# Seven quarter products in place of eight for the gate and up products of two swiglu stages

## The chip, the cores and the metric

The kernel runs on one core of a Trainium2 chip. The core has a matrix engine (TensorE, PE in the profile; its weight loads are listed apart as PEld), a vector engine (VectorE, DVE), a scalar engine (ScalarE, ACT), a general engine (GpSimd, POOL) and a sync engine that issues the weight transfers (SyncE, SP). Each engine works through its own list of instructions in order, and waits at an instruction until the semaphores that it names are set. The metric is device time in microseconds (us) of one execution; shown is the median of three runs.

## The reference

Two transformer blocks on 512 tokens of width 1024, in float32. Block 1 has two kinds of sparse attention and a squared-relu feed-forward; block 2 has a swiglu, a mixing stage (stick-breaking attention and an RWKV-7 recurrence), and a second swiglu. The change touches the two swiglus:

```python
def swiglu(x, w_gate, w_up, w_down):
    return (jax.nn.silu(x @ w_gate) * (x @ w_up)) @ w_down

x = x + FFN_HALF * swiglu(rms_norm_2(x, norm_ffn1[l]), ffn1_gate[l], ffn1_up[l], ffn1_down[l])
...
x = x + FFN_HALF * swiglu(rms_norm_2(x, norm_ffn2[l]), ffn2_gate[l], ffn2_up[l], ffn2_down[l])
```

`w_gate` and `w_up` are 1024 x 2816, `w_down` is 2816 x 1024.

## The kernel before

Activations lie transposed: eight tiles `x[0..7]` of 128 features by 512 tokens. Every float32 operand of a big product is split in two parts, an upper part rounded to the matrix format (ACT copies it: `whi`, `hh`, `vh`) and the rest as a lower part (DVE subtracts: `wlo`, `hl`, `vl`). A product is then three matmuls for each 128 x 128 block of weights: upper by upper, upper by the activations' lower part, lower by upper, in this order (`dense`, lines 352 to 360).

A swiglu stage (`swiglu`, lines 1410 to 1454) has 22 column groups of 128, each with one transfer of 1 MB (a unit): 1024 columns of gate and 1024 of up, 128 for each of the eight feature tiles. They come in three runs of 8, 8 and 6 units (`FFG`). A unit is 2 x 8 x 3 = 48 matmuls of 512 columns. Its two PSUM results are multiplied on DVE with the row scale `rr` (the norm's root, which is ready only some us after the stage begins, so the products run on unscaled activations), go through silu on ACT, are multiplied, and split into `vh` and `vl`. After each run come eight products with `w_down` (8 x 24, 24 or 18 matmuls), added into `x` on DVE.

The weights pass through the class `Stream`: two buffers of 1 MB (`NB = 2`), filled by SP in the order of use. A buffer is free again when the lower part of its last piece is done. `get` hands over one split piece of 1024 columns, and converts at most one further piece ahead (`LA = 1`); the split pieces lie in two buffers each of `whi` and `wlo`. Each engine's order is set by a scheduler ahead of the run, so an engine's list is not the order of the Python lines alone.

GpSimd has no instruction in the swiglu stages.

```python
            for _ in ks:
                if q == 0 and len(u) == 1:
                    for _ in steps:
                        pass
                    pg, pu = nx, self.bank("s")
                    self.dense(pu, ws.get(), h)
                else:
                    pg, pu = self.bank("mm"), self.bank("mm")
```

## Time and profile before

| | |
|---|---|
| median of three runs | 1954.82 us (1954.04 to 1955.6) |
| the profiled execution, its own time | 1951.49 us |
| its span from first to last instruction | 1949.7 us |
| mean granted TensorE clock | 0.979 of full speed |
| busy: PE, PEld | 1864.8 us (96%), 1456.1 us (75%) |
| busy: DVE, ACT, POOL | 1094.1 us (56%), 797.5 us (41%), 149.9 us (8%) |

Busy time is the time in which an engine had at least one instruction running. Matmuls are pipelined: the next starts before the one before has ended, so the time that one costs is the distance between starts, not its own length. The first swiglu lies from about 780 to 1134 us of the span, the second from about 1585 to the end.

### The profile page before, as it was taken

The page shows a single profiled execution, that of the slowest core. Times are in us where ns is not written, and L with a number is a line of the kernel's source. Part 1 is how long each engine was busy: PE and PEld are TensorE (multiplying, and loading weights), DVE is VectorE, ACT ScalarE, POOL GpSimd, SP SyncE. Part 2 cuts the span into 40 slices and gives each one's busy share as a digit, 9 for nine tenths or more (in the row PEclk, how much of TensorE's full clock was granted, in tenths as well). Part 3 has the DMA queues.
Part 4 walks back from the last instruction along what each step waited for, and adds up shares of the span by engine and source line. Part 5 has one row for each costly group of instructions (what it writes and reads, how often), then busy time and mean ns, then how long its engine had stood idle before and what let it go on. Part 6 is the DMA issues. An engine that isn't in the chain of part 4 may idle for free.

```text
span 1949.7 us, 27795 instructions
## 1 busy us (share of the span) xinstructions
PE 1864.8 (96%) x11552; PEld 1456.1 (75%) x11556; DVE 1094.1 (56%) x1843; ACT 797.5 (41%) x1385; POOL 149.9 (8%) x117
## 2 busy tenths in 40 slices
PE   5989999979999998999999999999999999999999
PEld 2766666758888886788888877776766778888887
DVE  7588875583434345543444556676667774444343
ACT  3666767343323233322322354343445753223231
POOL 4341110050000002000000000000001300000000
PEclk8999999889999998999999999999999999999999
DMA  7124214312223221222232231110100022222222
GB/s 300 57 87 140 78 65 152 113 61 92 103 90 105 89 106 65 87 93 101 88 107 87 89 124 55 45 45 24 40 18 33 22 87 96 99 92 103 92 98 92
DMA packets 27486, 171.56 MB, mean 88 GB/s; under 512 B 3168, under 2 KB 3680, under 8 KB 9184
## 3 DMA queue, kind: packets, MB, share of 16 engines
q1 hardware_dynamic: 23472, 163.44, 24.2%
q10 hardware_dynamic: 3888, 6.34, 1.0%
q8 instruction: 91, 1.49, 0.3%
q14 instruction: 35, 0.29, 0.0%
HBM read 167.67 MB, written 2.10 MB: 87 GB/s over the span
## 4 chain that ended last, share of the span: by engine, by line
PE 77%; DVE 3%; ACT 2%; POOL 1%; issue 1%; DMA 1%; ACTq 0%; POOLq 0%
PE ps_mm L339 43%; PE ps_s L339 23%; PE ps_c L339 5%; PE ps_pt L339 4%; PE ps_o L339 1%; ACT whi L243 1%; DVE wlo L249 1%; POOL xr L1332 0%; PE ps_pt L902 0%; POOL x L1381 0%; DMA mask<-in_mask 0%; DMA x<-in_x 0%; PE ps_mm L758 0%; DVE hl L1396 0%; DVE rs_v L510 0%
## 5 line engine op out<-in xcount | busy, mean ns | idle before, releaser
L243 ACT ACTIVATE whi<-w 128x1024 fp32r<-128x1024 f32 (+4 forms) x277 | 274.7, 994 | 740.7 <-PE ps_mm L339 440.8
L339 PE MATMUL ps_mm<-hh,whi 128*128 128x512 f32 x1304 | 519.9, 400 | 20.9 <-ACT whi L243 9.5
L339 PE MATMUL ps_mm<-hh,wlo 128*128 128x512 f32 x1304 | 518.1, 398 | 6.2 <-DVE wlo L249 6.2
L339 PE MATMUL ps_mm<-hl,whi 128*128 128x512 f32 x1304 | 519.2, 398 | 3.4 <-DVE hl L1339 2.0
L249 DVE TENSOR_TENSOR wlo<-w,whi 128x1024 fp32r<-128x1024 f32 (+7 forms) x316 | 322.3, 1025 | 149.3 <-ACT whi L243 148.8
L339 PEld LDWEIGHTS ps_mm<-hh,whi 128*128 128x128 f32 x1304 | 247.6, 190 | 82.3 <-ACT whi L243 12.8
L339 PEld LDWEIGHTS ps_mm<-hh,wlo 128*128 128x128 f32 x1304 | 247.4, 190 | 65.0 <-DVE wlo L249 10.1
L339 PEld LDWEIGHTS ps_mm<-hl,whi 128*128 128x128 f32 x1304 | 247.4, 190 | 60.3 <-DVE hl L1339 3.5
L339 PE MATMUL ps_s<-vl,whi 128*128 128x512 f32 x352 | 137.2, 390 | 0.0
L339 PE MATMUL ps_s<-vh,wlo 128*128 128x512 f32 x352 | 137.0, 389 | 0.0
L339 PE MATMUL ps_s<-vh,whi 128*128 128x512 f32 x352 | 136.6, 389 | 0.0
L1449 DVE SCALAR_TENSOR_TENSOR x<-ps_s,x 128x512 f32<-128x512 f32 x48 | 33.2, 692 | 129.2 <-PE ps_s L339 129.2
L1437 DVE TENSOR_TENSOR su<-ps_mm,rr 128x512 f32<-128x512 f32 x42 | 29.0, 691 | 133.1 <-PE ps_mm L339 133.1
L339 PE MATMUL ps_s<-uh,whi 128*128 128x512 f32 x256 | 99.6, 389 | 0.0
L339 PE MATMUL ps_s<-ul,whi 128*128 128x512 f32 x256 | 99.6, 389 | 0.0
L339 PE MATMUL ps_s<-uh,wlo 128*128 128x512 f32 x256 | 99.6, 389 | 0.0
L1436 DVE TENSOR_TENSOR sg<-ps_mm,rr 128x512 f32<-128x512 f32 x42 | 29.1, 692 | 97.3 <-PE ps_mm L339 93.2
L339 PEld LDWEIGHTS ps_s<-vl,whi 128*128 128x128 f32 x352 | 66.1, 188 | 14.3 <-DVE vl L783 0.7
L339 PEld LDWEIGHTS ps_s<-vh,wlo 128*128 128x128 f32 x352 | 66.1, 188 | 13.7
L339 PEld LDWEIGHTS ps_s<-vh,whi 128*128 128x128 f32 x352 | 66.1, 188 | 13.7
L876 ACT ACTIVATE P<-ps_s,st 128x512 f32<-128x512 f32 (+2 forms) x96 | 50.1, 528 | 15.7 <-DVE st L874 13.8
L1373 DVE TENSOR_TENSOR y<-y,ps_s 128x512 f32<-128x512 f32 x24 | 16.5, 688 | 70.0 <-PE ps_s L339 70.0
(576 smaller groups left out, 2762.5 us busy)
## 6 DMA issues: line engine op xcount, KB each, us to landing
w<-in_gu SPq DMA_DIRECT2D x44, 1024.0 KB, 4.8
w<-in_win SPq DMA_DIRECT2D x17, 1024.0 KB, 4.9
w<-in_wada SPq DMA_DIRECT2D x16, 1024.0 KB, 5.5
w<-in_wup SPq DMA_DIRECT2D x16, 1024.0 KB, 4.8
w<-in_wdn SPq DMA_DIRECT2D x16, 1024.0 KB, 4.8
w<-in_dn SPq DMA_DIRECT2D x16, 1024.0 KB, 4.8
wa<-in_wada SPq DMA_DIRECT2D x8, 1024.0 KB, 13.5
w<-in_dn SPq DMA_DIRECT2D x8, 768.0 KB, 4.2
```

The costliest lines, as they stand in the source:

```text
L243: self.nc.scalar.activation(hi[:, :n], src, AF.Copy)
L249: self.nc.vector.tensor_tensor(lo[:, o:m], src[:, o:m], hi[:, o:m], op=OP.subtract)
L339: self.last_pe = self.nc.tensor.matmul(o, l, r, start=start, stop=stop, skip_group_check=True)
L876: nc.scalar.activation(p[:, po:po + n], b[:, o:o + n], AF.Exp, bias=st[:, i:i + 1], accum_out=st[:, 4 + i:5 + i])
L1373: V.tensor_tensor(y[m], y[m], ps, op=OP.add)
L1436: V.tensor_tensor(g, pg, r, op=OP.mult)
L1437: V.tensor_tensor(v, pu, r, op=OP.mult)
L1449: V.scalar_tensor_tensor(self.x[m], ps, 0.5, self.x[m], op0=OP.mult, op1=OP.add)
```

## The change

The first three units of each swiglu stage stay as they were (`PLAIN = 3`). The other 19 take gate and up as one 2 x 2 block product: the weights of a unit are four quarters of 512 columns, A11 and A12 (gate, first and second four feature tiles), A21 and A22 (up), and the activations are four blocks, first and second four feature tiles by first and second 256 tokens. Seven products of quarter size take the place of eight. Of 48 matmuls of 512 columns come 7 x 4 x 3 = 84 of 256 columns.

The operands of the seven products are sums. Per unit GpSimd forms four weight sums of 512 columns (`combine`: S1, S2, S3, S4), from two SBUF tiles each. Once per stage, in the time of the plain units, `build` makes the activation operands in four steps: two scaled tiles on DVE (`h32`), four sums of 256 columns on GpSimd (`traw`, one buffer), three upper parts on ACT (`b1h`, `b2h`, `bth`) and three lower parts on DVE (`b1l`, `b2l`, `btl`: 256, 512 and 1024 columns). The scale `rr` is in them already, so the PSUM results need no multiplication with it. The results are put together from PSUM with three copies of 256 columns on ACT and three additions of 256 on DVE; the product with silu is two DVE instructions of 256. Weights are split in pieces of 512, seven a unit in place of two of 1024, up to four ahead (`LW = 3`), into the eight `hh`/`hl` tiles that held the activations of the plain units.

```diff
+PLAIN, LW = 3, 3
+            elif chunks == "W":
+                self.items += [(u, w, w == "A22") for w in ("A11", "A12", "S2", "S1", "S3", "S4", "A22")]
...
+    def combine(self, u):
+        if u in self.combos or self.sp is None:
+            return
+        q = lambda n: self.tiles[u][:, 512 * n:512 * n + 512]
+        s = self.combos[u] = {n: self.sp.tile([128, 512], F32, name="sw", tag="sw", bufs=4) for n in ("S1", "S2", "S3", "S4")}
+        for o, a, b, op in (("S1", q(2), q(3), OP.add), ("S2", s["S1"], q(0), OP.subtract), ("S3", q(0), q(2), OP.subtract),
+                            ("S4", q(1), s["S2"], OP.subtract)):
+            self.nc.gpsimd.tensor_tensor(s[o], a, b, op=op)
     def _convert(self):
-        while len(self.ready) <= self.la:
+        while True:
             while self.cp < len(self.items) and self.items[self.cp][1] is None:
                 self.cp += 1
             if self.cp >= len(self.items):
                 return
-            u, (off, n), last = self.items[self.cp]
-            if u >= self.dma_i:
+            u, ch, last = self.items[self.cp]
+            w = isinstance(ch, str)
+            if u >= self.dma_i or len(self.ready) > (LW if w else self.la) or w and self.sp is None:
                 return
-            src = self.tiles[u][:, off:off + n]
-            hi = self.phl.tile([128, 1024], F32R, name="whi")
-            lo = self.phl.tile([128, 1024], F32R, name="wlo")
+            if w:
+                self.combine(u)
+                a = ("A11", "A12", "A21", "A22")
+                src, n = self.tiles[u][:, 512 * a.index(ch):512 * a.index(ch) + 512] if ch in a else self.combos[u][ch], 512
+            else:
+                off, n = ch
+                src = self.tiles[u][:, off:off + n]
+            hi, lo = self.htile() if w else [self.phl.tile([128, 1024], F32R, name=n) for n in ("whi", "wlo")]
...
+            if ch == "S4" and isinstance(self.items[self.cp + 1][1], str) and u + 1 < self.dma_i:
+                self.combine(u + 1)
...
-                e += [(a[f"gu{n}"][u], c2) for u in ks]
+                e += [(a[f"gu{n}"][u], c2 if u < PLAIN else "W") for u in ks]
...
+    def seven_operands(self, pool, name, r):
+        V, S, P = self.nc.vector, self.nc.scalar, self.nc.gpsimd
+        two = lambda nm, *n: [pool.tile([128, 4, *n], F32R, name=nm + x) for x in "hl"]
+        b1, b2, t = two("b1", 256), two("b2", 512), two("bt", 4, 256)
+        def build(k):
+            hs = []
+            for m in (k, k + 4):
+                h = self.tmp("h32")
+                V.scalar_tensor_tensor(h, self.x[m], self.vec(name, m), r, op0=OP.mult, op1=OP.mult)
+                hs.append(h)
+            h1, h2 = hs
+            raw = pool.tile([128, 4, 256], F32, name="traw", tag="traw", bufs=1)
+            lo, hi = slice(0, 256), slice(256, 512)
+            P.tensor_tensor(raw[:, 0], h1[:, hi], h1[:, lo], op=OP.subtract)
+            P.tensor_tensor(raw[:, 1], h2[:, hi], raw[:, 0], op=OP.subtract)
+            P.tensor_tensor(raw[:, 2], h2[:, hi], h1[:, hi], op=OP.subtract)
+            P.tensor_tensor(raw[:, 3], h2[:, lo], raw[:, 1], op=OP.subtract)
+            for (oh, ol), src in ((b1, h1[:, lo]), (b2, h2), (t, raw)):
+                S.activation(oh[:, k], src, AF.Copy)
+                V.tensor_tensor(ol[:, k], src, oh[:, k], op=OP.subtract)
+        pick = lambda p, c: [(p[0][:, k][:, c], p[1][:, k][:, c]) for k in range(4)]
+        comb = lambda i: [(t[0][:, k, i], t[1][:, k, i]) for k in range(4)]
+        lo, hi = slice(0, 256), slice(256, 512)
+        ops = dict(P1=pick(b1, lo), P2=pick(b2, lo), P6=comb(1), P5=comb(0), P7=comb(2), P3=pick(b2, hi), P4=comb(3))
+        return ops, build
+    def seven(self, ops, x, z):
+        V, S, ws = self.nc.vector, self.nc.scalar, self.ws
+        lo, hi = slice(0, 256), slice(256, 512)
+        X, Y, Z = x[:, lo], x[:, hi], z[:, lo]
+        def prod(n, o, start=False):
+            wh, wl = ws.get()
+            for k, (xh, xl) in enumerate(ops[n]):
+                c = slice(128 * k, 128 * k + 128)
+                self.mm(o, wh[:, c], xh, start=start and k == 0)
+                self.mm(o, wh[:, c], xl)
+                self.mm(o, wl[:, c], xh, stop=k == 3)
+        s, s5, a, b = (self.tmp(n) for n in ("s12", "s5", "sg", "su"))
+        prod("P1", X, True)
+        S.activation(s[:, lo], X, AF.Copy)
+        prod("P2", Z, True)
+        V.tensor_tensor(a[:, lo], Z, s[:, lo], op=OP.add)
+        prod("P6", X)
+        S.activation(s[:, hi], X, AF.Copy)
+        prod("P5", Y)
+        S.activation(s5[:, lo], Y, AF.Copy)
+        prod("P7", X)
+        V.tensor_tensor(b[:, hi], X, s5[:, lo], op=OP.add)
+        prod("P3", Y)
+        V.tensor_tensor(a[:, hi], Y, s[:, hi], op=OP.add)
+        prod("P4", X)
+        return a, b, X
     def swiglu(self, h, out=None):
         tc, nc, ws = self.tc, self.nc, self.ws
         V, S = nc.vector, nc.scalar
         es = ExitStack()
         fp = es.enter_context(tc.tile_pool(name="fp2", bufs=1))
-        self.rpool = fp
+        self.rpool = ws.sp = fp
+        ws.htile = self.htile
         r = None
+        name = "norm_ffn1_2" if out is None else "norm_ffn2_2"
+        n = 0
         for q, ks in enumerate(FFG):
             u = []
             for _ in ks:
-                if q == 0 and len(u) == 1:
-                    for _ in steps:
-                        pass
-                    pg, pu = nx, self.bank("s")
-                    self.dense(pu, ws.get(), h)
+                n += 1
+                if n > PLAIN:
+                    g, v, X = self.seven(ops, self.bank("mm"), self.bank("s"))
+                    self.last_silu = S.activation(g, g, AF.Silu)
+                    V.tensor_tensor(v[:, :256], X, g[:, :256], op=OP.mult)
+                    V.tensor_tensor(v[:, 256:], v[:, 256:], g[:, 256:], op=OP.mult)
                 else:
-                    pg, pu = self.bank("mm"), self.bank("mm")
-                    if r is None:
-                        self.dense2(pg, pu, h)
-                        nx = self.bank("s")
-                        steps = self.dense_steps(h, ps=nx)
-                        r = self.gr(steps)
+                    if n == 2:
+                        build(0)
+                        for _ in steps:
+                            pass
+                        pg, pu = nx, self.bank("s")
+                        self.dense(pu, ws.get(), h)
+                        build(1)
                     else:
-                        self.dense(pg, ws.get(), h)
-                        self.dense(pu, ws.get(), h)
-                g, v = self.tmp("sg"), self.tmp("su")
-                V.tensor_tensor(g, pg, r, op=OP.mult)
-                V.tensor_tensor(v, pu, r, op=OP.mult)
-                self.last_silu = S.activation(g, g, AF.Silu)
-                V.tensor_tensor(v, v, g, op=OP.mult)
+                        pg, pu = self.bank("mm"), self.bank("mm")
+                        if r is None:
+                            self.dense2(pg, pu, h)
+                            nx = self.bank("s")
+                            steps = self.dense_steps(h, ps=nx)
+                            r = self.gr(steps)
+                            ops, build = self.seven_operands(fp, name, r)
+                        else:
+                            self.dense(pg, ws.get(), h)
+                            build(2)
+                            self.dense(pu, ws.get(), h)
+                            build(3)
+                    g, v = self.tmp("sg"), self.tmp("su")
+                    V.tensor_tensor(g, pg, r, op=OP.mult)
+                    V.tensor_tensor(v, pu, r, op=OP.mult)
+                    self.last_silu = S.activation(g, g, AF.Silu)
+                    V.tensor_tensor(v, v, g, op=OP.mult)
```

The scheduler gives these lists. First, the vector engine at the start of the first swiglu, from the first instruction that needs `rr_5935`. `w32_5848` is the third unit's weights, `wlo_5966` and `wlo_6006` (before), `wlo_5987` and `wlo_6042` (after) the lower parts of its gate and up halves; `h32`, `b1l`, `b2l`, `btl` belong to `build`. Before, from the second instruction that needs it:

```order
L1437 TENSOR_TENSOR su_5943<-ps_mm_5843,rr_5935 128x512
L1436 TENSOR_TENSOR sg_5993<-ps_s_5898,rr_5935 128x512
L249 TENSOR_TENSOR wlo_5966<-w32_5848,whi_5965 128x1024
L1439 TENSOR_TENSOR su_5943<-su_5943,sg_5942 128x512
L783 TENSOR_TENSOR vl_5949<-su_5943,vh_5948 128x512
L1437 TENSOR_TENSOR su_5994<-ps_s_5964,rr_5935 128x512
L1439 TENSOR_TENSOR su_5994<-su_5994,sg_5993 128x512
L249 TENSOR_TENSOR wlo_6006<-w32_5848,whi_6005 128x1024
```

After, from the first lower part of a build that needs a GpSimd sum:

```order
L1454 TENSOR_TENSOR btl_5947<-traw_5962,bth_5946 128x1024
L805 TENSOR_TENSOR vl_5955<-su_5949,vh_5954 128x512
L1443 SCALAR_TENSOR_TENSOR h32_6014<-x1_2989,vecs_80,rr_5935 128x512
L1443 SCALAR_TENSOR_TENSOR h32_6016<-x5_2993,vecs_80,rr_5935 128x512
L1454 TENSOR_TENSOR b1l_5943<-h32_6014,b1h_5942 128x256
L1534 TENSOR_TENSOR sg_6029<-ps_s_5898,rr_5935 128x512
L1454 TENSOR_TENSOR b2l_5945<-h32_6016,b2h_5944 128x512
L1535 TENSOR_TENSOR su_6030<-ps_s_5985,rr_5935 128x512
L1454 TENSOR_TENSOR btl_5947<-traw_6018,bth_5946 128x1024
L1537 TENSOR_TENSOR su_6030<-su_6030,sg_6029 128x512
L269 TENSOR_TENSOR wlo_6042<-w32_5848,whi_6041 128x1024
```

The lower part of the third unit's up half (`wlo_6006`, now `wlo_6042`) was the ninth instruction from the first that needs `rr`, and is now the nineteenth: it stands behind two builds, and so behind two `btl` that need sums from GpSimd.

Second, GpSimd at the same place. Before, its list goes from the last addition into `x` in block 1 to the attention of block 2, which is after the swiglu:

```order
L1381 TENSOR_TENSOR x4_2992<-x4_2992,y4_3011 128x512
L1381 TENSOR_TENSOR x5_2993<-x5_2993,y5_3012 128x512
L1381 TENSOR_TENSOR x6_2994<-x6_2994,y6_3013 128x512
L1381 TENSOR_TENSOR x7_2995<-x7_2995,y7_3014 128x512
```

After, the weight sums of the fourth unit (`w32_5921`) stand ahead of and between the first build's sums:

```order
L243 TENSOR_TENSOR sw_6047<-w32_5921 128x512
L243 TENSOR_TENSOR sw_6048<-sw_6047,w32_5921 128x512
L1448 TENSOR_TENSOR traw_5962<-h32_5958 128x256
L243 TENSOR_TENSOR sw_6049<-w32_5921 128x512
L1449 TENSOR_TENSOR traw_5962<-h32_5960,traw_5962 128x256
L1450 TENSOR_TENSOR traw_5962<-h32_5960,h32_5958 128x256
L1451 TENSOR_TENSOR traw_5962<-h32_5960,traw_5962 128x256
L243 TENSOR_TENSOR sw_6050<-w32_5921,sw_6048 128x512
L1448 TENSOR_TENSOR traw_6018<-h32_6014 128x256
```

So two sums that need the fourth unit's transfer come ahead of the first build, and the second build's sums wait for DVE to have read the first's from the one `traw` buffer.

Third, the vector engine within a run of seven-product units, about one unit's worth (after; `hl` is a weight's lower part, `sw` a GpSimd sum, the 256-wide rows with `ps_` read PSUM):

```order
L269 TENSOR_TENSOR hl_6556<-sw_6482,hh_6555 128x512
L805 TENSOR_TENSOR vl_6434<-su_6301,vh_6433 128x512
L269 TENSOR_TENSOR hl_6585<-sw_6481,hh_6584 128x512
L269 TENSOR_TENSOR hl_6602<-sw_6483,hh_6601 128x512
L269 TENSOR_TENSOR hl_6619<-sw_6484,hh_6618 128x512
L1487 TENSOR_TENSOR su_6442<-ps_mm_6437,s5_6440 128x256
L269 TENSOR_TENSOR hl_6644<-w32_6365,hh_6643 128x512
L1489 TENSOR_TENSOR sg_6441<-ps_mm_6437,s12_6439 128x256
L269 TENSOR_TENSOR hl_6663<-w32_6506,hh_6662 128x512
L1511 TENSOR_TENSOR su_6442<-su_6442,sg_6441 128x256
L1510 TENSOR_TENSOR su_6442<-ps_mm_6437,sg_6441 128x256
L1481 TENSOR_TENSOR sg_6582<-ps_s_6579,s12_6580 128x256
```

Weights of the next one or two units are converted between the additions that put a unit's result together.

## Rows read from the trace of the kernel before

**Rows 1.** The page: busy time, share of the span and instructions of each engine
```profile
PE 1864.8 (96%) x11552; PEld 1456.1 (75%) x11556; DVE 1094.1 (56%) x1843; ACT 797.5 (41%) x1385; POOL 149.9 (8%) x117
```

**Rows 2.** Chain that ended last, by time: start us, us, what; gate-and-up runs
```profile
796.70 65.28 PE ps_mm L339 x288
...
905.50 87.04 PE ps_mm L339 x384
...
1036.06 65.28 PE ps_mm L339 x288
...
1608.44 65.28 PE ps_mm L339 x288
```

**Rows 3.** One run by engine: PE, PEld, DVE, ACT, POOL, clock, DMA share, GB/s
```profile
905.00:992.00 87.00, 87.00 (x386) 72.03 (x385) 39.11 (x46) 25.57 (x31) 0.00 (x0) 1.00 0.29 97
```

**Rows 4.** Timeline of PE: first and last of thirty 348-column matmuls (start, us)
```profile
63.28 0.32 PE L339 MATMUL ps_s<-whi,hh 128*128 128x348 f32 x1
...
67.85 0.32 PE L339 MATMUL ps_o<-whi,hl 128*128 128x348 f32 x1
```

**Rows 5.** Timeline of PE: first and last of fifteen 32-column matmuls, weights changing
```profile
150.25 0.26 PE L339 MATMUL ps_s<-kcb,qst 128*128 128x32 f32 x1
...
151.82 0.26 PE L339 MATMUL ps_s<-kcb,qst 128*128 128x32 f32 x1
```

**Rows 6.** Timeline of PE: a 256-column matmul and its successor
```profile
1464.58 0.28 PE L339 MATMUL ps_c<-u,negones 128*128 128x256 f32 x1
1464.70 0.22 PE L339 MATMUL ps_c<-tok,negones 128*128 128x128 f32 x1
```

**Rows 7.** First swiglu, by shape: count | busy us, mean ns | idle before, releaser
```profile
L249 DVE TENSOR_TENSOR wlo<-w,whi 128x1024 fp32r<-128x1024 f32 x54 | 66.0, 1223 | 7.1 <-ACT whi L243 7.1
L243 ACT ACTIVATE whi<-w 128x1024 fp32r<-128x1024 f32 x55 | 58.4, 1062 | 204.6 <-PE ps_mm L339 135.3 <-PE ps_s L339 67.4 <-issue 1.9
L782 ACT ACTIVATE vh<-su 128x512 fp32r<-128x512 f32 x20 | 12.7, 634 | 13.6 <-DVE su L1439 13.6
```

**Rows 8.** Timeline of POOL, two successors; then one line's min/median/max ns
```profile
61.27 1.29 POOL L813 TENSOR_TENSOR rp_t<-rp_t,rp_s 128x512 f32<-128x512 f32 x1
62.51 1.30 POOL L812 TENSOR_TENSOR rp_s<-rp_s,sin 128x512 f32<-128x512 f32 x1
...
L1564 POOL TENSOR_TENSOR u<-tmt,u x2: 744/832/919, 1455.5 to 1519.7; 128x256 fp32r<-128x256 f32 x2
```

**Rows 9.** Timeline of POOL, then DVE, where both are busy
```profile
410.00 13.71 POOL L1344 TENSOR_TENSOR x<-x,y 128x512 f32<-128x512 f32 x8
...
412.21 2.54 DVE L1362 TENSOR_TENSOR relu<-relu 128x512 f32<-128x512 f32 x2 [0.86 <-ACT relu L1361]
414.68 2.28 DVE L249 TENSOR_TENSOR wlo<-w,whi 128x1024 fp32r<-128x1024 f32 x1
416.88 3.44 DVE L783 TENSOR_TENSOR ul<-relu,uh 128x512 fp32r<-128x512 f32 x2
420.25 2.32 DVE L249 TENSOR_TENSOR wlo<-w,whi 128x1024 fp32r<-128x1024 f32 x1
```

**Rows 10.** Timelines of ACT and DVE around the scale's arrival, both stages
```profile
790.59 0.60 ACT L1407 ACTIVATE rr<-ps_pt 128x512 f32<-128x512 f32 x1 [1.90 <-PE ps_pt L339]
...
784.90 1.22 DVE L249 TENSOR_TENSOR wlo<-w,whi 128x1024 fp32r<-128x1024 f32 x1
786.04 0.68 DVE L573 TENSOR_TENSOR st<-st,sq 128x512 f32<-128x512 f32 x1
...
791.22 0.69 DVE L1436 TENSOR_TENSOR sg<-ps_mm,rr 128x512 f32<-128x512 f32 x1 [1.94 <-ACT rr L1407]
791.83 0.68 DVE L1437 TENSOR_TENSOR su<-ps_mm,rr 128x512 f32<-128x512 f32 x1
...
798.08 1.22 DVE L249 TENSOR_TENSOR wlo<-w,whi 128x1024 fp32r<-128x1024 f32 x1
...
1600.28 0.60 ACT L1407 ACTIVATE rr<-ps_pt 128x512 f32<-128x512 f32 x1 [2.77 <-PE ps_pt L339]
```

**Rows 11.** The page: DMA issues (count, KB each, us from issue to landing)
```profile
w<-in_gu SPq DMA_DIRECT2D x44, 1024.0 KB, 4.8
```

More of the change, by code (lines that the diff above doesn't have):

```diff
@@ L221, in __init__ @@
         self.pool = 0
+        self.sp, self.combos, self.htile = None, {}, None
     def load(self):
@@ L1453, in swiglu @@
                     nc.scalar.dma_start(out[m], self.x[m])
+        ws.sp = None
         es.close()
```

## The prediction

> **What bounds the kernel now.** I read the busy times first: the matrix engine is at work for 96% of the span, and no other engine comes near [rows 1]. Then the chain of waits, in order of time. The reader is to see that a run of gate and up products stands in it as one unbroken piece of matmuls: 288, 384 and 288 in the first swiglu, and the same three again in the second [rows 2]. 65.28 / 288 and 87.04 / 384 both give 226.7 ns a matmul, or 48 x 0.2267 = 10.88 us a unit. Third, one run by engine: in 87 us TensorE is busy throughout at its full clock (1.00, the 2.4 GHz level), DVE for 39.1, ACT for 25.6, GpSimd not at all [rows 3]. So within a run only matmuls count, and the other engines have room. At the beginning of a stage the margin is smaller, because the row scale arrives late [rows 10].
>
> **The matmuls.** 38 units change (19 in each of two stages). Each gives up 48 matmuls of 512 columns for 84 of 256. No stream of 256-column matmuls is in the trace, so I bound the price. A stream of 348 columns with a weight change at each runs at (67.85 - 63.28) / 29 = 157.6 ns [rows 4]. With 226.7 ns at 512 this is a line of 0.4212 ns a column and a fixed part of 11 ns, which gives 118.8 ns at 256. From below: a fixed part of nothing, half of 226.7 = 113.3. From above: the whole excess of 226.7 over 213.3 (512 columns at 2.4 GHz) as a fixed part, 106.7 + 13.4 = 120. A single one among others takes 0.12 us [rows 6]. Does the weight load set a floor? With 32 columns and a new weight block each time the distance is (151.82 - 150.25) / 14 = 112 ns [rows 5]; that is the load's pace, and lies just under all three. I take 119: 84 x 0.119 = 10.0 us a unit, 0.88 less than now, 33.6 us over 38 units (52 and 30 at the ends).
>
> The Trainium skill (TensorE: Matmul & The Clock Gate, section Back-to-back issue gap) gives a gap of N / 2.4 + 2.5 ns; by it 256 columns would take 109 ns, a unit 9.2, and the whole change 65 us less. It also gives 216 ns for 512, where this trace has 226.7, so its fixed part is too small here and the sum does not use it.
>
> **The other engines within a run.** DVE's instructions follow each other at 0.61 us for 512 columns (791.22 to 791.83) and 1.14 for 1024 (784.90 to 786.04) [rows 10], so about 0.35 for 256. A unit now has eight of 512 and one of 256 with both inputs in SBUF (seven lower weight parts, the split of the result, one half of the product with silu): 5.2 us. Four of 256 read PSUM: 1.4. GpSimd's four sums of 512 take 1.24 each (61.27 to 62.51) [rows 8]: 5.0. ACT has twelve instructions of at most 0.63 [rows 7], 7.6 us. Each alone fits beside 10.0.
>
> But DVE and GpSimd hinder each other. From 410.00 to 423.71 eight sums on GpSimd take 1.71 us each in place of 1.24, and DVE's instructions from 412.21 to 422.57 take 10.36 us for four of 512 and two of 1024, which alone are 4.7 [rows 9]. In those 10.36 us GpSimd did 6.05 sums, worth 7.5. Work of 12.2 us fitted into 10.36: the two run nearly by turns, at a factor of 0.85. For a unit that is (5.2 + 5.0) x 0.85 = 8.7 us, still under 10.0, and instructions that read PSUM can run beside GpSimd. So TensorE stays the bound in a run. For late pieces (a product that waits until DVE has read its bank) I add 0.1 a unit: 10.1, a gain of 38 x 0.78 = 29.8 us.
>
> The Trainium skill (SBUF — State Buffer, section Who interferes with whom) says that a vector instruction with two SBUF inputs contends with a GpSimd instruction that reads SBUF, and that the loser fully blocks. By that rule the factor is 1, not 0.85; what it does to the time is the third case below.
>
> **The start of a stage.** Here the change puts work on the path. The order lists show it: the third unit's last lower part (`wlo_6042`) stands behind two builds on DVE, these wait for ACT's `bth`, and that for four sums on GpSimd, ahead of which stand the fourth unit's sums. The latter are ready in time: the second unit's buffer is free at 784.90 + 1.22, and 4.8 us for its refill [rows 11] is 791. What is queued behind on ACT are the upper weight parts, on DVE all that follows, and TensorE waits for both.
>
> With no hindrance between the engines, in the first stage: scale at 791.2; S1, S2, S3 and four build sums of 0.75 [rows 8] bring GpSimd to 797.7; `bth` 1.06, `btl` 1.14, `vl`, two `h32`, three more sums, `bth`, `btl`, the product with silu and `wlo_6042` end at 808.1. Before, that part was done at 799.3 [rows 10] and TensorE needs it 0.45 us after 796.70 + 5.44 = 802.14 [rows 2], so 5.5 us late. The third and fourth build follow in the same way (`h32`, three sums, `bth`, `btl`, and once more), and the last `bth` is there at 819.5. TensorE needs it for the fourth block of the third product, at 807.58 + 33 x 0.119 = 811.5: 8.0 us lost. The path takes 28.3 us from the scale; in the second stage, from 1600.88, it ends at 1629.2, needed at 1608.44 + 10.88 + 3.93 = 1623.3: 5.9 lost. Together 13.9, the low end.
>
> By turns: until that point GpSimd has 16 sums of 0.75 and five of 1.24, 18.2 us; DVE has eight `h32`, two weight parts of 1024, four `b1l`, four `b2l`, three `btl`, two products, two splits and three pieces of 512 with two SBUF inputs, 18.7. At 0.85 the 36.9 us are 31.4; with the last `bth` the stages come to 823.7 and 1633.3, 12.1 and 10.0 late. At a factor of 1 it is 17.6 and 15.6, the high end of 33.2. I take 0.85, as measured where both are busy: 22.1. For the first seven-product unit, whose next lower parts DVE has not begun, 1.2 a stage: 2.4. The later runs of a stage start with their first sums made beside the products with `w_down`, where DVE has time, so I cost that at nothing; without that cover it would be about 5 us a run.
>
> **Sum.** 29.8 - 22.1 - 2.4 = 5.3 us less than the profiled execution's 1951.5: 1946.2. The median of the runs lies 3.3 higher, so 1949.5, say 1950.
>
> **Rivals.** First, faster: the engines hinder each other less, as GpSimd's sums fall into DVE's waits. Starts then cost 13.9, and units come at 10.0: 33.6 - 13.9 = 19.7 less, 1935; with 0.116 a matmul, 1925. For it: all engines wait on each other at a start, so they are seldom both busy. Against it: DVE has no idle time left there, as the 18.7 us show.
>
> Second, slower: strict turns. A unit needs 10.2 us of DVE and GpSimd in turn, and of the 1.4 us that read PSUM a fifth falls outside GpSimd's time, 10.5. The gain shrinks to 38 x 0.38 = 14.4, starts cost 33.2 + 2.4: 21 us longer, 1976. It decides from a unit of 10.2 on, where with my starts the gain is gone. For it: a DVE instruction of 1.14 took 2.3 beside GpSimd [rows 9]. Against it: the factor that those same rows give. The rule of the skill above is this case; with all PSUM reads hidden (10.2 a unit) it gives 1965.
>
> Third, no change within what can be told: the starts cost what the units gain, 1955.
>
> Fourth, the weight load is the bound at its recorded length rather than at its pace. A unit of 84 x 0.19 would be 16 us and the kernel about 190 us slower. Rows 5 speak against it: loads follow each other at 112 ns.
>
> **How the numbers follow.** A difference of 0.2% (3.9 us) is about what the measurement can tell from none. My forecast has 0.42, with its own range from 1943 to 1957: faster 0.24, same 0.13, slower 0.05. Less hindrance has 0.22, all faster. Strict turns have 0.29: slower 0.28, same 0.01. No change 0.05, the load 0.02. Faster 0.46, same 0.19, slower 0.35. The range that leaves out 0.1 at each side reaches from the middle of the faster case to that of the slower one, 1932 to 1976.
>
> **What will show it.** In the new profile, the distance of 256-column matmuls within a run (119 ns; under 113 or over 121 and the first term is wrong). A unit's length in the second run (10.1 us, from 10.5 on the rival). GpSimd's sums of 512 (1.5 to 1.7 us beside DVE; 1.25 and they don't meet). TensorE's idle time between the third unit's gate half and the fourth block of the third product (12 and 10 us; if it is under 7 in both stages, the start was priced too high). And `wlo_6042` as the releaser of TensorE in the middle of it. If idle time of TensorE lies spread over the runs instead, with DVE as its releaser, the second case holds.

## The result: 53 us slower, and the profile after

The changed kernel takes 2007.92 us (median of four runs, 2003.76 to 2011.09) beside 1954.59 for the kernel before on the same chip: 1.0271 times as long, 95% interval 1.0251 to 1.0291. The forecast was 1950 with a range of 1932 to 1976, so it was wrong in sign, and the time lies outside the range. The profiled execution has a span of 2007.4 us, 57.7 more than before.

First the page's busy times, then five stretches by engine: 87 us of the second run, and four pieces of the start of the first swiglu (columns as in [rows 3]).

```profile
PE 1881.5 (94%) x12920; PEld 1511.1 (75%) x12924; DVE 1288.3 (64%) x2149; ACT 922.1 (46%) x1713; POOL 430.1 (21%) x301
```

```profile
936.00:1023.00 87.00, 86.13 (x663) 81.14 (x662) 63.25 (x96) 45.30 (x87) 42.47 (x26) 1.00 0.27 98
805.00:810.00 5.00, 0.73 (x2) 0.30 (x2) 5.00 (x8) 1.88 (x3) 2.88 (x3) 0.81 0.00 0
810.00:815.00 5.00, 0.00 (x0) 0.00 (x0) 3.22 (x5) 2.21 (x3) 0.89 (x2) 0.50 0.00 0
815.00:820.00 5.00, 4.98 (x15) 3.99 (x16) 4.57 (x7) 2.97 (x6) 1.44 (x2) 0.66 0.64 210
825.00:830.00 5.00, 3.25 (x13) 2.96 (x14) 3.48 (x6) 1.77 (x3) 3.85 (x4) 0.52 0.00 2
```

Within a run TensorE looks as busy as in [rows 3], 86.1 of 87 us, though it loses time: short waits hide between matmuls that overlap. At the start it stands still, and its clock falls to 0.50.

To see where the time went, I took three distances from ACT's timeline, in which every unit leaves one `vh`: from the scale `rr` to the eighth unit's `vh` (start), from there to the sixteenth's (second run, with the first down phase) and to the last (third run). Before they are 72.95 and 75.00 (two stages), 130.56 and 109.59. The two ends of the first start: the eighth `vh` of the kernel before (its `rr` stands in [rows 10]), then `rr` and the eighth `vh` of the changed kernel:

```profile
863.54 0.63 ACT L782 ACTIVATE vh<-su 128x512 fp32r<-128x512 f32 x1 [0.63 <-DVE su L1439]
...
793.00 0.60 ACT L1429 ACTIVATE rr<-ps_pt 128x512 f32<-128x512 f32 x1 [1.90 <-PE ps_pt L361]
...
891.03 0.63 ACT L804 ACTIVATE vh<-su 128x512 fp32r<-128x512 f32 x1 [1.53 <-DVE su L1510]
```

The table has the median and its ratio to the kernel before, timed beside it, and what each kernel's profiled execution took more in the three distances (first / second stage).

| kernel | median us | ratio (95%) | start | second run | third run |
|---|---|---|---|---|---|
| changed | 2007.9 | 1.0271 (1.0251-1.0291) | +25.1 / +23.6 | +2.0 / +1.1 | +1.2 / +0.6 |
| e1 no weight sums | 1986.4 | 1.0153 (1.0136-1.0170) | +19.3 / +15.5 | -1.2 / -0.9 | -1.6 / -1.4 |
| e2 other bank | 2019.8 | 1.0326 (1.0309-1.0343) | +22.9 / +21.9 | +4.0 / +3.8 | +2.1 / +2.7 |
| e9 own bank | 2016.2 | 1.0299 (1.0277-1.0320) | +24.7 / +22.1 | +5.9 / +3.7 | +2.2 / +2.5 |
| e5 copies first | 2032.6 | 1.0394 (1.0373-1.0415) | +26.6 / +25.1 | +8.5 / +7.9 | +4.5 / +4.3 |
| e6 other bank, copies first | 2000.1 | 1.0225 (1.0205-1.0246) | +20.0 / +18.5 | +2.4 / +1.2 | -0.6 / -1.1 |
| e10 own bank, copies first, six ahead | 1986.6 | 1.0146 (1.0119-1.0172) | +20.2 / +17.7 | -1.3 / -4.7 | -1.7 / -3.8 |
| e3 five plain units | 2002.0 | 1.0237 (1.0222-1.0252) | +20.5 / +21.7 | +1.0 / +1.2 | +0.8 / +1.1 |
| e4 no build sums | 1993.4 | 1.0189 (1.0174-1.0205) | +16.8 / +17.5 | +1.2 / +1.0 | +1.2 / +1.0 |
| e7 builds spread | 1994.0 | 1.0200 (1.0183-1.0216) | +17.8 / +18.1 | +1.2 / +0.9 | +0.5 / +0.5 |
| e13 builds in parts | 1962.0 | 1.0032 (1.0020-1.0043) | +0.0 / -0.0 | +4.8 / +3.2 | +1.1 / +1.0 |
| e8 e6 and e7 | 1981.2 | 1.0129 (1.0111-1.0148) | +11.0 / +11.4 | +0.5 / +1.7 | +0.5 / -1.1 |
| e12 all | 1939.2 | 0.9916 (0.9898-0.9934) | +0.0 / +0.0 | -6.0 / -6.0 | -2.9 / -4.3 |
| e15 e12, no weight sums | 1934.7 | 0.9884 (0.9860-0.9909) | +0.0 / -0.0 | -7.4 / -7.4 | -5.1 / -5.6 |
| e16 e12, six plain units | 1949.5 | 0.9959 (0.9944-0.9973) | +2.0 / +1.8 | -4.2 / -4.8 | -3.9 / -2.5 |

So 48.7 of the changed kernel's 57.7 us lie in the two starts and 4.9 in the runs; the other 4.1 lie outside these stretches, where the work is the same and other executions come to other values (`rr` of the first stage at 790.1 to 796.4 us).

**A unit.** ACT's timeline, `vh` of successive units of the second run:

```profile
948.13 0.63 ACT L804 ACTIVATE vh<-su 128x512 fp32r<-128x512 f32 x1
958.80 0.61 ACT L804 ACTIVATE vh<-su 128x512 fp32r<-128x512 f32 x1
970.05 0.63 ACT L804 ACTIVATE vh<-su 128x512 fp32r<-128x512 f32 x1
```

10.67 and 11.25 in turn, 10.96 on average; forecast 10.1. The timeline of TensorE beside one copy shows why:

```profile
948.81 0.38 ACT L1483 ACTIVATE s<-ps_mm 128x256 f32<-128x256 f32 x1
...
949.09 0.28 PE L361 MATMUL ps_mm<-b1l,hh 128*128 128x256 f32 x1
949.25 0.19 PEld L361 LDWEIGHTS ps_mm<-bth,hh 128*128 128x128 f32 x1
949.25 0.39 PE L361 MATMUL ps_mm<-bth,hh 128*128 128x256 f32 x1
...
949.47 0.28 PE L361 MATMUL ps_mm<-btl,hh 128*128 128x256 f32 x1
```

The pace is 0.12 us, as forecast. But P5 (`bth` at 949.25) writes Y and waits until ACT has read X, the other half of its PSUM tile (948.81 + 0.38). Its weights are loaded only then, so 0.14 us are lost for a wait of 0.04. The longest wait of a pair of units, in the chain of waits:

```profile
951.79 0.62 ACT hh L263
...
952.44 1.53 DVE hl L269
953.98 0.34 DVE su L1487
...
954.36 1.70 PE ps_mm L361 x12
```

P3 also writes Y, and waits for DVE's read of X (`su`, L1487), which stands in DVE's queue behind a lower part (`hl`) that takes 1.53 in place of 0.69 beside GpSimd.

**The start.** The chain of waits in the first stage (some small pieces left out):

```profile
788.56 4.85 DMA w<-in_gu
...
793.57 1.32 POOL sw L243
...
797.84 2.27 POOL sw L243
...
803.31 1.07 ACT bth L1453
...
804.40 1.23 DVE btl L1454
...
807.04 1.11 POOL traw L1448
...
810.92 1.06 ACT bth L1453
...
813.83 1.15 DVE wlo L269
...
815.02 2.09 PE ps_mm L361 x4
```

It is the path of the forecast, link by link: weight sums, build sums, `bth`, `btl`, the next build, `wlo_6042`. All is 2.4 us later than in the trace of before, as `rr` is (793.00, there 790.59). TensorE waits 8.4 us at `wlo_6042` by the waits of this stretch, and 3.0 at a `b2h` (823.5 to 826.5).

In both waits the granted clock falls from 1.00 to 0.50, its level of 1.2 GHz, and TensorE works at 0.50 for some time after each. From 815.02 to 818.50 eight distances between matmul starts take 3.48 us (8 x 0.2267 is 1.81), from 827.33 to 830.70 sixteen take 3.37 (16 x 0.12 is 1.92): 3.1 us together, 3.6 in the second stage by the same reading. Before, the clock is 1.00 throughout both starts. That all of this reaches the end of the start is not shown.

**A first unit after a down phase** takes 12.6 to 13.6 us (57.10 - 43.52 in the first stage's second run; 43.52 is a down phase, 192 x 0.2267). The chain there:

```profile
918.04 1.28 POOL sw L243
...
921.72 4.45 DVE hl L269 x4
926.17 0.60 DVE x L1547
926.77 1.14 DVE wlo L269
...
927.96 2.14 PE ps_s L361 x8
```

Four lower parts of the next run, which wait for GpSimd's sums, stand in DVE's queue ahead of the addition into `x` and of `wlo` for the down phase itself.

### The profile page after: what moved, and what is told of

It reads as the page before. It is cut to its first block, busy times and chain, and to the rows that moved or that the text cites. A ratio compares the mean times of both kernels' runs of the same rounds, so it can differ in the third digit from the quotient of the medians.

```text
span 2007.4 us, 31607 instructions
## 1 busy us (share of the span) xinstructions
PE 1881.5 (94%) x12920; PEld 1511.1 (75%) x12924; DVE 1288.3 (64%) x2149; ACT 922.1 (46%) x1713; POOL 430.1 (21%) x301
## 3 DMA queue, kind: packets, MB, share of 16 engines
q1 hardware_dynamic: 23472, 163.44, 22.9%
## 4 chain that ended last, share of the span: by engine, by line
PE 65%; DVE 9%; POOL 4%; ACT 4%; DMA 2%; issue 2%; ACTq 0%; POOLq 0%; SPq 0%
PE ps_mm L361 35%; PE ps_s L361 20%; PE ps_c L361 5%; PE ps_pt L361 4%; DVE hl L269 3%; POOL sw L243 1%; DMA w<-in_gu 1%; DVE wlo L269 1%; ACT hh L263 1%; PE ps_o L361 1%; ACT whi L263 1%; POOL xr L1354 0%; DMA w<-in_dn 0%; PE ps_pt L924 0%; POOL traw L1450 0%
## 5 line engine op out<-in xcount | busy, mean ns | idle before, releaser
L269 DVE TENSOR_TENSOR wlo<-w,whi 128x1024 fp32r<-128x1024 f32 (+6 forms) x240 | 230.3, 968 | 140.8 <-ACT whi L263 140.5
L361 PE MATMUL ps_mm<-hh,whi 128*128 128x512 f32 x696 | 285.5, 412 | 23.7 <-ACT whi L263 12.3
L361 PE MATMUL ps_mm<-hh,wlo 128*128 128x512 f32 x696 | 283.6, 408 | 20.4 <-DVE wlo L269 20.4
L361 PE MATMUL ps_mm<-hl,whi 128*128 128x512 f32 x696 | 284.4, 409 | 3.4 <-DVE hl L1361 1.9
L243 POOL TENSOR_TENSOR sw<-w 128x512 f32<-128x512 f32 x76 | 123.5, 1625 | 331.8 <-DMA w<-in_gu 289.1
L361 PE MATMUL ps_mm<-bth,hh 128*128 128x256 f32 x608 | 182.8, 301 | 6.2 <-ACT s L1485 3.0
L361 PEld LDWEIGHTS ps_mm<-hh,whi 128*128 128x128 f32 x696 | 134.4, 194 | 62.5 <-ACT whi L263 16.4
L361 PE MATMUL ps_mm<-btl,hh 128*128 128x256 f32 x608 | 171.4, 282 | 0.0
L361 PE MATMUL ps_mm<-bth,hl 128*128 128x256 f32 x608 | 169.3, 282 | 0.0
L269 DVE TENSOR_TENSOR hl<-sw,hh 128x512 fp32r<-128x512 f32 x152 | 140.2, 942 | 36.2 <-ACT hh L263 33.6
L269 DVE TENSOR_TENSOR hl<-w,hh 128x512 fp32r<-128x512 f32 x114 | 113.7, 1011 | 21.9 <-ACT hh L263 18.9
L361 PEld LDWEIGHTS ps_mm<-btl,hh 128*128 128x128 f32 x608 | 116.1, 191 | 0.0
```

What stands on the lines that cost most here:

```text
L243: self.nc.gpsimd.tensor_tensor(s[o], a, b, op=op)
L269: self.nc.vector.tensor_tensor(lo[:, o:m], src[:, o:m], hi[:, o:m], op=OP.subtract)
L361: self.last_pe = self.nc.tensor.matmul(o, l, r, start=start, stop=stop, skip_group_check=True)
```

## Experiments

### What holds a unit at 10.96 us

e1 has `self.combos[u] = {"S1": q(2), "S2": q(0), "S3": q(1), "S4": q(3)}` in place of GpSimd's four instructions.

> Leaves out GpSimd's four weight sums a unit: the seven products take quarters of the weights as they are (the output is not the reference's); conversions, matmuls, copies and additions stay as they are, and so do GpSimd's sums in the four builds. In the changed kernel a unit of the second run takes 10.96 us where 84 matmuls at 0.12 are 10.1, and the first unit after a down phase takes 12.6 to 13.6. Theory 1, hindrance (GpSimd's sums slow DVE's lower parts from 0.69 to as much as 1.53 us, and TensorE waits for them): units of 10.2, the first unit after a down phase 10.5 to 11, so per stage 14 x 0.75 + 4 less and some 3 at the start: 1970 to 1980. Theory 2, PSUM (a product that writes one half of a bank waits until the other half has been read): units stay at 10.7 to 10.9, only the first units after a down phase get shorter: 1995 to 2000.

21.5 us less by the medians, but mid-run units only go to 10.37 and 11.25 in turn, 10.81. So hindrance is 0.15 of a unit's 0.86; the rest of the gain came at the starts and first units. Neither theory had both halves.

```diff
# e2
-        X, Y, Z = x[:, lo], x[:, hi], z[:, lo]
+        X, Y, Z = x[:, lo], z[:, hi], z[:, lo]
# e9
+        X, Y, Z = x[:, lo], y[:, lo], z[:, lo]      # y = self.bank("o"); P5 starts it
```

> Puts the block Y of each unit (products P5 and P3) beside Z in Z's PSUM bank and no longer beside X. Nothing else changes. In the changed kernel P5 and P3 wait for reads of X, because X and Y are halves of one PSUM tile. Theory 2, PSUM: with Y in the other bank a unit of the second run falls from 10.96 to 10.2 or 10.3 us; 28 units that run steadily x 0.7 gives 1985 to 1990. Theory 1, hindrance: DVE's lower parts stay late, units stay above 10.7, time within 6 us of 2007.

> Y in a PSUM bank of its own (the one tagged o, which has no other use in a run); order, sums and builds as in the changed kernel. P5 and P3 then wait for no read of X or Z. Theory 2, PSUM alone: units fall from 10.96 to 10.2 to 10.4, 1988 to 1992. Theory 3, ACT's queue: P6's wait for the copy of P1, behind a conversion that waits for a weight tile, stays at about 1 us a unit as with Y in Z's bank; units 11.1 to 11.4, 2010 to 2020.

Units take 11.3 to 11.6 us on average in both, against 10.96; e2 is slower than the changed kernel, e9 too by the medians, though their intervals meet. e9 is what theory 3 expected, e2 what neither did. (In the profiled executions of e9 and e6 the clock also fell to 0.50 for some 3.4 us in the first stage's second run, which is part of their +5.9 and +2.4.) All short waits are gone and one long one a unit has come. ACT's timeline in e2, where P6 starts at 973.84:

```profile
972.36 0.63 ACT L804 ACTIVATE vh<-su 128x512 fp32r<-128x512 f32 x1 [1.77 <-DVE su L1510]
972.90 0.61 ACT L263 ACTIVATE hh<-w 128x512 fp32r<-128x512 f32 x1
973.42 0.36 ACT L1479 ACTIVATE s<-ps_mm 128x256 f32<-128x256 f32 x1
```

P6 needs the copy of P1 (L1479), which stands behind the previous unit's `vh`, itself late from DVE, and a conversion. I had put this down to a conversion that waits for a weight tile; the row shows that ACT waited for DVE, and that `hh` followed at once. The queue was right, its head was not.

```diff
# e5, e6 (with e2's bank), e10 (with e9's bank and LW = 5)
-            self.nc.scalar.activation(hi[:, :n], src, AF.Copy)
+            with self.tc.issue_after(self.gate.ins) if w and self.gate else ExitStack():
+                self.nc.scalar.activation(hi[:, :n], src, AF.Copy)
...
+        ws.gate = S.activation(s[:, lo], X, AF.Copy)   # so at all three copies
```

> ACT's conversions of weight quarters may no longer be placed ahead of the copies from PSUM that stand before them in the code (banks, sums and builds as in the changed kernel). In the run with Y in the other bank every unit had one wait of 1.0 to 1.3 us of the product P6 for ACT's copy of P1, and that copy stood in ACT's queue behind a conversion that waited for TensorE to release a weight tile. Without GpSimd's weight sums a unit still took 10.81 us, so hindrance is some 0.15 of the 0.86 that a unit is over my forecast. Theory 2, PSUM (P5 and P3 wait for reads of the other half of their bank): units stay at 10.7 to 10.9, time 1998 to 2007. Theory 3, ACT's queue (copies late behind conversions): units fall to 10.2 to 10.5, 1985 to 1993.

> Y in Z's bank, and ACT's conversions behind the copies. If theories 2 and 3 are each half of it (the bank takes away the waits of P5 and P3, the order the wait of P6), a unit of the second run comes to 10.1 to 10.3 us, and 28 steady units x 0.7 give 1985 to 1990. If hindrance between GpSimd and DVE is what is left, units are at 10.5 and the time is 1995 or more.

e5 is the slowest of all, units of some 12.1. Its chain of waits, the same in each unit:

```profile
971.87 0.39 ACT s L1485
...
972.30 1.70 PE ps_mm L363 x12
...
974.09 0.39 ACT s L1487
...
974.52 6.30 PE ps_mm L363 x48
```

In this order P6, P5 and P7 follow one another directly on TensorE; in the changed kernel five matmuls of another unit's product stand between P6 and P5 (948.61 to 949.09). So P5 waits for the copy of X behind P6 (L1485), though it writes Y, the other half of the tile, and P7 for that of Y behind P5 (L1487). The matmuls start 0.75 and 0.81 after the one before, and the next ones 0.22: 1.5 of the about 2.0 us over 10.08. Why the order takes the other product away was not taken apart; now and then a conversion that comes only after a copy makes DVE's read `su` late too (989.02, 0.35 after the matmul before). With Z's bank (e6) units are still 11.4. e5 missed both expectations; e6 has the time of its second case (1995 or more), but not its unit (10.5).

> Y in a bank of its own, ACT's conversions no longer ahead of the copies that stand before them in the code, and up to six split pieces ahead in place of four (LW = 5), so that the order does not make conversions late. Theories 2 and 3 together: nothing that TensorE needs stands behind something that waits for TensorE; units 10.2 to 10.4 us, 28 x 0.65 less than the changed kernel: 1986 to 1992. Hindrance, or DVE's own queue, as what is left: units of 10.7 or more, 2000 or more.

As expected: 1986.6, units of 10.24, TensorE's starts 0.12 apart with 0.16 us lost a unit (10.24 - 10.08). Own bank, order and lookahead together do it; with bank alone or order alone units are longer. Lookahead alone, and with one of the other two, was not tried, nor own bank and order without it, so which of the three are needed stays open.

### What the start costs

> Five plain units at the beginning of each stage in place of three; the four builds stay where they are in the code (beside the second and third unit). The start of a stage costs some 25 us in the changed kernel, of which 10.6 are one wait for the third unit's last lower part (wlo_6042, behind two builds in DVE's queue). Theory A, due time (the builds are late for their first use): the wait of 10.6 stays, the rest (about 14 a stage) is gone, as builds three and four have 20 us more: 1975 to 1982. Theory B, work (DVE and GpSimd have more to do at the changeover than fits, whenever it comes): the loss behind the wait moves to the sixth unit, 2000 or more.

> Leaves out GpSimd's four sums in each build: the parts bth and btl are made from the scaled tiles themselves in two pieces of 512 columns each (the output is not the reference's). The weight sums of the units stay. DVE has as much to do as before or 0.1 us more a build. Theory A, chain through GpSimd (h32, four sums, bth, btl, one traw buffer, so each build takes a full round of three engines): wlo_6042 is ready some 8 us earlier, the wait of 10.6 falls to 2 to 4, and builds three and four come 5 us earlier: 10 to 14 us a stage less, 1980 to 1988. Theory B, DVE's own work is the bound at the start: at most 4 us a stage less, 2000.

e3 sets `PLAIN = 5` and leaves the builds where they are; e4 replaces `traw` by `h1` and `h2`. e3 gained 4.6 and 1.9 us a stage: theory B's number, and the loss did move, to the fifth unit's `vh` (15.1 us after the fourth's). e4 gained 8.2 and 6.1: GpSimd's part of the chain is a quarter to a third, less than theory A and more than theory B said.

```diff
# e7: PLAIN = 6, the four calls of build taken out of the units' halves
+                    if 2 <= n <= 5:
+                        build(n - 2)
```

> Six plain units a stage, and one build in each of the second to the fifth, after that unit's products; the rest as in the changed kernel. With five plain units and the builds unmoved the start was only some 4 to 5 us a stage shorter, so the wait of the third unit's lower part and the changeover both cost. Theory A, builds bunched in DVE's queue ahead of lower parts that TensorE waits for: spread over four units (3.4 us of DVE each beside 4.1 of 10.88) they cost nothing, a start costs 0 to 4 us in place of 25, 1960 to 1968. Theory B, the changeover itself (first conversions, first weight sums, GpSimd beside DVE) costs: 10 to 14 us a stage remain, 1978 to 1985.

It missed theory A by 30 us and theory B by 9. The chain of waits of a plain unit with a build:

```profile
796.27 0.69 DVE su L1531
796.97 0.66 DVE h L1443
797.63 0.60 DVE su L1533
798.23 1.14 DVE h L1443
799.37 0.34 DVE b1l L1454
799.71 1.15 DVE vl L805
800.85 1.15 DVE b2l L1454
802.00 1.68 DVE wlo L269
...
803.72 5.30 PE ps_mm L361 x22
```

The first two such units take 12.8 us, each 1.75 longer at one matmul that waits for `wlo`. DVE is not full over a unit (3.4 for the build by my count, and 39.1 / 8 = 4.9 by [rows 3], of 10.88), but a split weight tile is released only when its piece's matmuls end, and the next piece's lower part is due 5.44 + 0.45 us later. In that window DVE had 7.4 us of work up to the end of `wlo` (796.27 to 803.68), instructions of 512 columns at 1.1 to 1.2 beside GpSimd in place of 0.6 to 0.7. At their lengths alone they would be some 5.2 us (six of 512 at 0.6 to 0.7, 0.34 and 1.14), so GpSimd's share in this wait is not separated from the window's. The larger part of what e7's start costs lies behind, where theory B put it: the wait at the fourth build is 4.3 us, and the `vh` of the sixth unit, the last plain one, comes 20.6 us after the fifth's.

```diff
# e13: PLAIN = 8, sums on DVE, build as a generator of three parts, builds in units 3, 5, 7, 8
+                            for j in todo.get(2 * n, ()):       # after the gate half
+                                next(builds[j])
...
+                    for j in todo.get(2 * n + 1, ()):           # after the products
+                        next(builds[j])
```

> Eight plain units a stage; builds in units 3, 5, 7 and 8, each in three parts: the scaled tiles and the four sums (on DVE, not GpSimd) beside the gate half, b1 and b2 after the unit's products, bt beside the next gate half. The rest is the changed kernel. With one whole build after a unit, each of those units took 12.8 us in place of 10.88: TensorE waited 1.75 us for a lower part, because between the release of a weight tile and the first use of the next piece there are only some 5.9 us, and DVE had 7.4 us of work in them. Theory window (work must fit each half unit, not the average): with 4.4 to 5.0 us of DVE a half unit the starts cost 0 to 3 a stage; 14 units at 10.96 and two first units after a down phase at 2 each: 1963 to 1970. Theory work (whenever it is done, the builds and the changeover cost 10 or more a stage): 1980 or more.

1962.0, just under what theory window expected, and the starts cost 0.03 and -0.01 us; the clock stays at 1.00. The same sums, more of the work on DVE, are free here. But e13 differs from e7 in three things: the builds come in parts, over more units, and without GpSimd. Each of them can lighten a window, and no run separates them. The changeover now lies at the first down phase and costs 5.5 and 3.9 there (59.86 and 58.27 - 43.52 - 10.88).

### Together

> The three edits together: builds spread over plain units two to five with six plain units a stage, Y in Z's bank, ACT's conversions behind the copies. If they are independent, 16 units a stage at 10.2 in place of 10.88 give 22 us back, the two starts and the four first units after a down phase cost 4 to 8 together: 1936 to 1945, faster than the kernel before. If what is left is hindrance (10.5 a unit) and a start of 5 each: 1955 to 1962.

> Builds in parts beside eight plain units, Y in its own bank, conversions behind the copies with six pieces ahead, and in a down phase the lower parts of the next run's weights behind the additions into x on DVE. If the three theories (window at the start, shared bank, queue order) are what cost the 53 us, 14 units a stage run at 10.2 to 10.4, starts and first units cost 0 to 3 a stage: 1938 to 1950, below the kernel before (1954.5). If GpSimd's sums hinder DVE so that units stay at 10.7 or more: 1955 to 1962.

e8 (e6 with e7) missed, since both its halves did. e12 is e13 with e10, and in a down phase the lower parts of the next run's weights are issued behind the additions into `x`. As expected it beats both kernels: 1939.24 beside 1956.45, 0.9916 (0.9898 to 0.9934). ACT's timeline:

```profile
948.77 0.63 ACT L807 ACTIVATE vh<-su 128x512 fp32r<-128x512 f32 x1 [1.73 <-DVE su L1519]
...
959.01 0.63 ACT L807 ACTIVATE vh<-su 128x512 fp32r<-128x512 f32 x1 [1.74 <-DVE su L1519]
959.55 0.37 ACT L1486 ACTIVATE s<-ps_mm 128x256 f32<-128x256 f32 x1
```

Units are 10.24 apart, and the copy now follows `vh` directly. The 0.16 us left is P6's wait for this copy: its first matmul starts 0.18 and the next 0.22 after the one before (959.97, 960.19). The first unit after the first down phase takes 10.9 (54.42 - 43.52), after the second 11.9; the new order in the down phase was tried only together with the rest.

> The version with all edits, with GpSimd's weight sums left out (quarters in their place; the output is not the reference's). Theory hindrance (GpSimd's sums slow DVE, and that reaches TensorE): units fall below the 10.24 us of the version with the sums, towards 10.08, the first units after a down phase lose 1 us: 1928 to 1934. Theory cover (queues once in order, a slower DVE is hidden): within 4 us of 1939.

The units are those of the first theory, 10.08 us, 84 x 0.120, with no matmul late, so GpSimd's sums cost 0.16 a unit, as in e1; the time lies between the two ranges. By the table the sums cost 6.3 us in all once the queues are in order (25.5 below before in place of 19.2), where leaving them out of the changed kernel gave 23.9 by the same table. So the larger part of that was not the hindrance itself.

```profile
938.37 0.63 ACT L804 ACTIVATE vh<-su 128x512 fp32r<-128x512 f32 x1 [0.83 <-DVE su L1516]
948.45 0.63 ACT L804 ACTIVATE vh<-su 128x512 fp32r<-128x512 f32 x1 [0.82 <-DVE su L1516]
```

> The version with all edits, with six plain units a stage in place of eight and the builds in units 3 to 6. Two more seven-product units a stage gain 2 x 0.64 us each, 2.6 us in all: 1936 to 1938 if the changeover inside a run costs no more than at a down phase. Rival: at the changeover inside a run the first weight sums stand ahead of DVE's reads (three lower parts that wait for GpSimd), 3 to 6 us a stage: 1942 to 1950.

The rival came: the `vh` of its fifth and sixth unit come 12.3 and 15.0 us after the one before. A changeover inside a run costs more than two units gain; why DVE's queue costs that there was not taken apart.

## Why the prediction was wrong, point by point

- **The matmuls**: right. 0.12 us each; e15's unit is 10.08 where I had 10.0. The floor by the weight load did not show.
- **"So TensorE stays the bound in a run. For late pieces ... I add 0.1 a unit"**: the step that failed in the runs. With 19 units a stage at 10.1, the runs after the first should have given back 21.8 us (28 x 0.78); they took 4.9 more, 26.7 off. I had compared each engine's work with a unit's time and looked at no queue or PSUM tile. Two things of one kind showed in their place: products that wait for a read of the other half of their tile, and reads that stand in an engine's queue behind work of another unit. e10 took both away, with more lookahead, and the unit was 10.24.
- **Hindrance**: seen, and mis-sized only as a rival. GpSimd's sums take 1.58 to 1.74 us on average in the second run, as forecast for being beside DVE. The timelines of POOL and DVE show it:

```profile
951.67 1.75 POOL L243 TENSOR_TENSOR sw<-sw,w 128x512 f32<-128x512 f32 x1
953.39 1.73 POOL L243 TENSOR_TENSOR sw<-w 128x512 f32<-128x512 f32 x1
```

```profile
951.58 0.69 DVE L269 TENSOR_TENSOR hl<-sw,hh 128x512 fp32r<-128x512 f32 x1 [1.15 <-ACT hh L263]
952.44 1.53 DVE L269 TENSOR_TENSOR hl<-sw,hh 128x512 fp32r<-128x512 f32 x1 [0.17 <-ACT hh L263]
```

In 1.53 us DVE did work of 0.6 and GpSimd 1.53 / 1.74 of a sum that alone takes 1.24, 1.09: 1.69 in 1.53, a factor of 0.9 in this place; over the whole 87 us an estimate of the same kind gives 27.3 / (12.9 + 16.5), 0.93. The Trainium skill (SBUF — State Buffer, section Who interferes with whom) lets the loser fully block, a factor of 1. The trace is near it. e15 shows what hindrance costs: 0.16 a unit, not the 0.4 of my slower rival. That rival came closest in time (1976) and had the wrong mechanism. Its sign, waits of TensorE spread over the runs with DVE as releaser, did come in part (`su`, L1487): the sign did not tell the order of a queue from slow instructions.
- **"The later runs of a stage start with their first sums made beside the products with `w_down`, ... so I cost that at nothing"**: failed. By the chain of waits DVE's work had time there, but stood in the wrong order; 1.6 to 2.6 us a run over a mid-run unit.
- **The start**: the path was right, its price far too low. Five seven-product units in the first run should have saved 3.9, so the starts lost 29.0 and 27.5; I had 13.3 and 11.2 (12.1 and 10.0, with 1.2 for the first unit). In the first stage, less the 2.4 us by which all is later, the first build's sums on GpSimd end at 800.9, not 797.7, `wlo_6042` at 812.6, not 808.1 (both without hindrance), and the last `bth` at 827.9 (829.19 + 1.07 - 2.4), where I had 819.5 without hindrance and 823.7 with. So TensorE's operand is 16.4 us late for 811.5 by the forecast's own reading, where I had 12.1, and 12.6 of the 29.0 come behind it, where I had 1.2: the first two seven-product units take 15.5 and 11.7 us. Three things failed. I summed work by engine with a factor of 0.85 and took DVE to have no idle time, but the work goes round three engines with one `traw` buffer: DVE waits 1.7 to 1.8 us for three of the four `bth`, GpSimd 5.5 for an `h32`. I took the loss as ended with the last `bth`, while DVE still had the next units' lower parts to make up. And the sum had no term for the clock, which cost TensorE 3.1 and 3.6 us in the two starts. How the 15.7 and 16.3 divide between the first two was not measured. e13 shows starts that cost nothing with the same sums to make.

The errors add up: 15.7 + 16.3 at the starts, 26.7 in the runs and 4.1 outside are 62.8; 57.7 + 5.3 = 63.0 were to be explained.

## What to carry to other kernels

A share of busy time says that work fits on average. What decided here was the window between the release of a buffer and the first use of its next content, 5.9 us, and what is queued on the engine in that window, in order. Before adding products that share a PSUM tile or an engine's queue with reads of earlier ones, list for each wait of the bounding engine what stands ahead of its releaser. Try such repairs together as well as alone: in the runs own bank or order alone made units longer (1.030 and 1.039 beside 1.027 in time), both with more lookahead gave 1.015, and with the start's repair, which alone gave 1.003, 0.992.

## What the hardware showed that I had not expected

- A short wait cost more than itself: after a wait of 0.04 us the weight load began with the matmul (both at 949.25), and 0.14 us were lost in all.
- TensorE's granted clock fell from 1.00 to 0.50 (its level of 1.2 GHz) in the wait of 8.4 us before 815.02, and was at 1.00 again from about 818.5, with TensorE at work from 815.02 on (0.66 in 815 to 820). It fell again after the wait of 3.0 us that ended at 826.52 (0.52 in 825 to 830) and came back about 832. So TensorE paid for these waits twice, as idle time and in slow matmuls.
